# A convolution that also gathers its layer norm's sums, a norm's transpose moved into the next head, and a softmax difference in one VectorE operation

## The chip, the core and the metric

The kernel runs on one core of a Trainium2 chip. A core has TensorE (PE in the profile, its weight loads PEld), VectorE (DVE), ScalarE (ACT), GpSimd (POOL) and SyncE (SP, which here issues most DMAs). Each engine works through its own list of instructions in order and waits on semaphores for the others. The working memory is SBUF; TensorE writes to PSUM, 8 banks of 128 x 512 fp32 words each; DRAM holds inputs, outputs and what does not fit. The metric is the device time of one execution, in microseconds (us); lower is better.

## The reference, cut to what matters

One layer on 1024 tokens of 1024 channels, fp32:

```
h = rms_norm(x, g_pre);  proj = h @ w_in          # 1024 x 9216
glu_in, gate_a, q, k, v, gate_b, merge = split(proj)
u   = a * sigmoid(b)                              # a, b = halves of glu_in
u   = depthwise_causal_conv(u, 31 taps) + conv_b
y_a = (silu(layer_norm(u, ln_g, ln_b)) * silu(gate_a)) @ w_conv_proj
for 8 heads, 8 blocks of 128 queries:             # rotary on q, k; chunk mask
    p0, p1 = softmax(q0 k0), softmax(q1 k1)
    o = (p0 - lam * p1) @ v
y_b = (rms_norm(o, g_subln) * c * silu(gate_b)) @ w_attn_proj
y   = sigmoid(m_a) * y_a + sigmoid(m_b) * y_b
out = x + rms_norm(y @ w_out, g_post)
```

The layer norm is over the channels of one token, so it needs the convolution of all 1024 channels before any of it can be finished.

## The kernel before

Channels lie on partitions, 8 blocks of 128; tokens lie along the free dimension in two halves of 512. Every fp32 matrix product is made of two-part splits: a factor is cast to a reduced format (ACT) and the rest subtracted from it (POOL), and `product` (L242) does three matmuls of 128 x 512 for each of 4 slices, 12 for a product.

**Stage 1, the input projection.** Two 128-column blocks of `w_in` make a pair; there are 32 pairs, and `PLAN` (L63) lists them: u (both halves of the gated unit, block i), q (queries and keys), s and g (the two SiLU gates), v, m (merge gate of the convolution branch). A pair is done in Strassen's manner with 7 products ("steps") where 8 would be usual. `quarters` is that sequence: a step fills a PSUM bank of tag "g" (6 banks), then DVE's `plus` (L524) combines the bank with a running sum in one of 7 SBUF buffers ("cmb"), and a `use_...` function takes each finished quarter further, mostly by way of small tiles of 128 x 512. The factors of the next pair are made meanwhile (`factors`, `made`: ACT casts, POOL sums and differences, 8 buffers "wf"). For the first three pairs the two products that need no later data are begun beforehand (`begin_pair`), so these pairs have 5 steps left.

All small tiles come from `small()`, a ring of 6 buffers of one tag. They are handed out in the order in which the program is written: the n-th small tile can be written only when the (n-6)-th has been read for the last time.

**The convolution.** When both halves of u block i are there, `conv(i)` is written at the end of `quarters` for that pair. It is 31 DVE operations of 128 x 1024, one per tap: the first (L445) starts an accumulator in PSUM, 29 go on with it and the last (30 operations at L448) writes the result to an SBUF tile of its own, `cv`, which is stored to DRAM; POOL adds it to a running total (L455). The whole of it stands under a priority offset that tells the scheduler to slip the taps in where DVE would have nothing else.

**The layer norm.** PLAN's tokens l0 to l4. l0 and l1 (`ln_half`) read the stored convolution again, subtract the mean that a matmul with a constant matrix gives (L477), store the difference to `cc`, square it and add up (L472 among them). l2 (`ln_rows`) turns the sums into reciprocal roots by way of DRAM. l3 and l4 (`ln_out`) read `cc` and the stored gate `ga` back, multiply, apply SiLU and store `zd`.

**Stage 2, attention.** 8 heads of 8 query blocks in pairs (j). Per block: score matmuls (L839, L840), row maxima (DVE), exponentials (ACT, L852), then the difference of the two maps: reciprocal factors (DVE, L859), ACT scales the second map (L861), POOL adds it to the first (L862); TensorE transposes the result (L868), and after every two blocks it is multiplied with v (L881). Pieces of other products fill gaps (`filling`: `merge_gate`, L707, `conv_out`, `attn_out`). At a head's end the roots of its norm are computed, transposed on TensorE (L900), and stored; the next head's j = 0 reads them back and multiplies (`norm_head`).

**Stage 3** is the output projection, the last norm and the residual.

The scheduler orders each engine's instructions once, at build time, by the priorities and its own model; what stands in a queue below is that fixed order.

Of the kernel before, what the change touches and what calls it, by code (L numbers as in the profile page):

```python
# [40 lines left out]
def weight_blocks():  # L41
# [11 lines left out]
    for name, off in (("v", OFF_V), ("a", OFF_A), ("b", OFF_B), ("ga", OFF_GA), ("gb", OFF_GB),  # L53
# [10 lines left out]
        "m0 m1 l0 l1 g2 m2 l2 g3 l3 m3 l4")  # L64
# [3 lines left out]
def block_kernel(ctx, tc, x, positions, vecs, conv_w, lambdas, g_subln, g_post,  # L68
# [32 lines left out]
    def psum_g():  # L101
        return ps.tile(hb, F32, name="ps_g", tag="g", bufs=6)
# [205 lines left out]
    lam = const.tile([P, 4], F32, name="lam")  # L308
# [132 lines left out]
    def conv(i):  # L441
        u = conved[i]
        acc = ps.tile(blk, F32, name="cacc", tag="cv", bufs=1)
        a = wide("cv", "cv", 1)
        nc.vector.tensor_scalar(out=acc, in0=u[:, 0:T], scalar1=cw[:, i, 0:1], scalar2=vec[:, 1, i:i + 1],  # L445
                                op0=ALU.mult, op1=ALU.add)
        for k in range(1, TAPS):
            nc.vector.scalar_tensor_tensor(out=a if k == TAPS - 1 else acc, in0=u[:, k:k + T],  # L448
                                           scalar=cw[:, i, k:k + 1], in1=acc, op0=ALU.mult, op1=ALU.add)
        nc.sync.dma_start(out=cv_dram[i], in_=a)  # L450
        if i == 0:
            ln["tot"] = wide("tot", "tot", 1)
            nc.gpsimd.tensor_copy(out=ln["tot"], in_=a)
        else:
            nc.gpsimd.tensor_tensor(out=ln["tot"], in0=ln["tot"], in1=a, op=ALU.add)  # L455


    def ln_half(hh):

        sl = halves[hh]  # L460
        both = ps.tile(blk, F32, name="mu_tot", tag="cv", bufs=1)
        mu, tot = both[:, :HALF], both[:, HALF:]
        nc.tensor.matmul(mu, ones_d, ln["tot"][:, sl], start=True, stop=True)
        for i in range(8):
            c = small("cvr")
            nc.sync.dma_start(out=c, in_=cv_dram[i][:, sl])
            nc.vector.tensor_tensor(out=c, in0=c, in1=mu, op=ALU.subtract)
            nc.sync.dma_start(out=cc_dram[i][:, sl], in_=c)
            sq = small("csq") if i else tot
            nc.scalar.activation(out=sq, in_=c, func=AF.Square)  # L470
            if i:
                nc.vector.tensor_tensor(out=ln["tot"][:, sl] if i == 7 else tot, in0=sq, in1=tot, op=ALU.add)  # L472

    def ln_rows():
        for hh in range(2):
            pm = psum_g()
            nc.tensor.matmul(pm, ones_d, ln["tot"][:, halves[hh]], start=True, stop=True)  # L477
            row = small("row")
            nc.scalar.copy(out=row[0:1, :], in_=pm[0:1, :])
            nc.sync.dma_start(out=var_dram[:, halves[hh]], in_=row[0:1, :])  # L480
        vcol = tmp_pool.tile([P, 8], F32, name="vcol", bufs=1)
        vr = tmp_pool.tile([P, 8], F32, name="vr", bufs=1)
        nc.sync.dma_start(out=vcol, in_=var_dram.rearrange("o (a b) -> (o a) b", b=8))
        nc.vector.tensor_scalar(out=vcol, in0=vcol, scalar1=EPS, scalar2=None, op0=ALU.add)
        rsqrt_small(vcol, vr)
        nc.sync.dma_start(out=rs_dram.rearrange("o (a b) -> (o a) b", b=8), in_=vr)
        ln["rs"] = ps.tile(blk, F32, name="rs", tag="cv", bufs=1)
        for hh in range(2):
            rs = small("rs")
            nc.sync.dma_start(out=rs, in_=rs_dram[:, halves[hh]].broadcast_to([P, HALF]))  # L490
            nc.scalar.copy(out=ln["rs"][:, halves[hh]], in_=rs)

    def ln_out(tiles):
        for i in tiles:
            for hh in range(2):
                sl = halves[hh]
                c, g = small("cvz"), small("gaz")
                nc.sync.dma_start(out=c, in_=cc_dram[i][:, sl])
                nc.sync.dma_start(out=g, in_=ga_dram[i][:, sl])
                nc.vector.tensor_tensor(out=c, in0=c, in1=ln["rs"][:, sl], op=ALU.mult)  # L500
                nc.scalar.activation(out=c, in_=c, func=AF.Silu, scale=vec[:, 2, i:i + 1],
                                     bias=vec[:, 3, i:i + 1])
                nc.vector.scalar_tensor_tensor(out=c, in0=c, scalar=0.5, in1=g, op0=ALU.mult, op1=ALU.mult)
                nc.sync.dma_start(out=z_dram[i][:, sl], in_=c)
# [102 lines left out]
    def psum_2():  # L607
        return ps.tile(hb, F32, name="ps_r", tag="r", bufs=3)
# [202 lines left out]
    def head(h, loaded_head):  # L811
# [5 lines left out]
        for j in range(4):  # L817
# [3 lines left out]
            for u in range(2):  # L821
# [39 lines left out]
                nc.scalar.activation(out=es[1][:, :n], in_=es[1][:, :n], func=AF.Copy, scale=rz[:, 1:2])  # L861
                nc.gpsimd.tensor_tensor(out=es[0][:, :n], in0=es[0][:, :n], in1=es[1][:, :n], op=ALU.add)  # L862
# [37 lines left out]
        nc.tensor.transpose(out=rt[0:8, 0:P], in_=r, identity=ident)  # L900
# [3 lines left out]
        return nxt  # L904
# [163 lines left out]
```

## Time and profile before

| | us |
|---|---|
| median of 2 runs | 1429.84 (1429.42 to 1430.25) |
| profiled execution | 1432.29 |
| its span | 1430.5 |
| PE busy | 1218.6 (85%) |
| DVE busy | 929.1 (65%) |
| POOL busy | 805.4 (56%) |
| ACT busy | 577.4 (40%) |
| mean granted TensorE clock | 0.934 |

In the rows below, a group or a timeline line names engine, line of the kernel, operation, output<-inputs and shape; "x30" is how many there are of it; "[25.05 <-DVE tot L472]" is the time for which the engine had been idle ahead of it and what released it. A row of the windows gives a stretch, its length, the busy time of PE, PEld, DVE, ACT and POOL with the number of instructions, the granted clock, the DMA share and GB/s.

### The profile page before, as it was taken

The page shows a single profiled execution, that of the slowest core. Times are in us where ns is not written, and L with a number is a line of the kernel's source. Part 1 is how long each engine was busy: PE and PEld are TensorE (multiplying, and loading weights), DVE is VectorE, ACT ScalarE, POOL GpSimd, SP SyncE. Part 2 cuts the span into 40 slices and gives each one's busy share as a digit, 9 for nine tenths or more (in the row PEclk, how much of TensorE's full clock was granted, in tenths as well). Part 3 has the DMA queues.
Part 4 walks back from the last instruction along what each step waited for, and adds up shares of the span by engine and source line. Part 5 has one row for each costly group of instructions (what it writes and reads, how often), then busy time and mean ns, then how long its engine had stood idle before and what let it go on. Part 6 is the DMA issues. An engine that isn't in the chain of part 4 may idle for free.

```text
span 1430.5 us, 17209 instructions
## 1 busy us (share of the span) xinstructions
PE 1218.6 (85%) x5672; PEld 1006.9 (70%) x5672; DVE 929.1 (65%) x1485; ACT 577.4 (40%) x1127; POOL 805.4 (56%) x644
## 2 busy tenths in 40 slices
PE   3799999998999999995740799987899888979998
PEld 2578777877888877783530588876788777758686
DVE  4879998998999999234442253455645456635733
ACT  7543342332333323332331464465534555513311
POOL 4798798989888876765200333366433466745000
PEclk9899999999999999998775799987999989989999
DMA  6123434544333243444389653746657385557522
GB/s 211 62 90 113 159 137 136 171 145 142 131 103 113 101 153 135 162 153 149 122 287 246 189 148 133 191 123 218 183 177 192 121 239 160 171 172 262 170 97 88
DMA packets 98492, 223.76 MB, mean 156 GB/s; under 512 B 12274, under 2 KB 12738, under 8 KB 98404
## 3 DMA queue, kind: packets, MB, share of 16 engines
q1 hardware_dynamic: 95364, 212.95, 47.1%
q0 software_dynamic: 2320, 7.49, 1.8%
q10 hardware_dynamic: 720, 2.23, 0.4%
q8 instruction: 45, 0.74, 0.2%
q14 instruction: 43, 0.35, 0.1%
HBM read 150.23 MB, written 72.39 MB: 156 GB/s over the span
## 4 chain that ended last, share of the span: by engine, by line
PE 30%; DMA 12%; DVE 5%; ACT 3%; issue 3%; POOL 1%; SPq 1%; DVEq 0%; ACTq 0%; POOLq 0%
PE ps_g L665 8%; PE ps_g L707 5%; PE ps_r L881 3%; PE ps_s L839 2%; PE ps_s L840 2%; PE ps_o L989 2%; PE ps_o L990 2%; PE ps_o L991 2%; DMA cvr<-cv 2%; PE ps_o L665 2%; PE ps_r L868 1%; DMA ql<-qkl 1%; DMA gaz<-ga 1%; DMA qh<-qkh 1%; DMA yar<-yab 1%
## 5 line engine op out<-in xcount | busy, mean ns | idle before, releaser
L242 PE MATMUL ps_g<-T,wf 128*128 128x512 f32 x1536 | 362.2, 391 | 6.0 <-DVE u L524 5.6
L242 PEld LDWEIGHTS ps_g<-T,wf 128*128 128x128 f32 x1536 | 289.1, 189 | 68.1 <-DVE u L524 5.2
L242 PE MATMUL ps_g<-B,wf 128*128 128x512 f32 x1152 | 286.9, 402 | 20.4 <-DVE c L524 15.3
L448 DVE SCALAR_TENSOR_TENSOR cacc<-u,cw,cacc 128x1024 f32<-128x1024 f32 x232 | 297.5, 1282 | 2.9
L242 PEld LDWEIGHTS ps_g<-B,wf 128*128 128x128 f32 x1152 | 221.9, 194 | 72.8 <-DVE c L524 18.9
L183 POOL TENSOR_TENSOR wf<-wraw,wf 128x512 fp32r<-128x512 f32 x128 | 173.9, 1363 | 56.5 <-ACT wf L182 56.5
L862 POOL TENSOR_TENSOR e<-e 128x128 f32<-128x128 f32 (+3 forms) x64 | 91.1, 1424 | 139.5 <-ACT e L861 83.4
L183 POOL TENSOR_TENSOR wf<-wsum,wf 128x512 fp32r<-128x512 f32 x96 | 129.0, 1344 | 41.6 <-ACT wf L182 41.3
L643 POOL TENSOR_TENSOR wL<-wraw,wH 128x512 fp32r<-128x512 f32 x48 | 61.7, 1303 | 140.9 <-ACT wH L642 128.3
L707 PE MATMUL ps_g<-B,wH 128*128 128x512 f32 x256 | 84.2, 406 | 59.4 <-ACT wH L642 57.5
L852 ACT ACTIVATE e<-ps_s,nm 128x256 f32<-128x256 f32 (+7 forms) x128 | 94.8, 743 | 56.1 <-DVE nm L849 24.6
L182 ACT CAST wf<-wraw 128x512 fp32r<-128x512 f32 x128 | 78.2, 618 | 94.8 <-PE ps_g L242 78.7
L707 PEld LDWEIGHTS ps_g<-B,wH 128*128 128x128 f32 x256 | 48.6, 194 | 70.1 <-ACT wH L642 58.0
L524 DVE SCALAR_TENSOR_TENSOR u<-ps_g,u 128x512 f32<-128x512 f32 x96 | 65.6, 684 | 49.4 <-PE ps_g L242 49.4
L182 ACT CAST wf<-wsum 128x512 fp32r<-128x512 f32 x96 | 59.3, 618 | 92.0 <-PE ps_g L242 48.4
L839 PE MATMUL ps_s<-kst,qh 128*128 128x384 f32 (+4 forms) x192 | 72.3, 383 | 15.4 <-ACT e L852 12.2
L840 PE MATMUL ps_s<-kst,ql 128*128 128x384 f32 (+4 forms) x192 | 69.0, 365 | 2.1 <-DMA ql<-qkl 2.1
L871 DVE TENSOR_TENSOR wtL<-ps_r,wtH 128x512 fp32r<-128x512 f32 (+2 forms) x96 | 51.3, 551 | 27.2 <-ACT wtH L870 26.8
L849 DVE TENSOR_REDUCE nm<-ps_s 128x1 f32<-128x640 f32 (+3 forms) x64 | 65.2, 1020 | 1.4
L204 POOL TENSOR_TENSOR wsum<-wraw 128x512 f32<-128x512 f32 x32 | 43.0, 1344 | 38.3 <-DMA wraw<-w_in 34.4
L861 ACT ACTIVATE e<-e,rz 128x128 f32<-128x128 f32 (+3 forms) x64 | 49.7, 779 | 25.4 <-DVE rz L859 23.8
L665 PE MATMUL ps_g<-zH,wH 128*128 128x512 f32 x128 | 52.7, 411 | 7.1 <-DVE tar L690 3.4
(227 smaller groups left out, 2378.6 us busy)
## 6 DMA issues: line engine op xcount, KB each, us to landing
wraw<-w_in SPq DMA_DIRECT2D x67, 512.0 KB, 3.8
qkh<-qkH SPq DMA_DIRECT2D x32, 256.0 KB, 2.9
qkl<-qkL SPq DMA_DIRECT2D x32, 256.0 KB, 3.2
qh<-qkh SPq DMA_DIRECT2D x32, 256.0 KB, 7.9
ql<-qkl SPq DMA_DIRECT2D x32, 256.0 KB, 8.8
tbr<-tb SPq DMA_DIRECT2D x32, 256.0 KB, 3.3
sg<-th SPq DMA_DIRECT2D x16, 256.0 KB, 2.4
cv<-cv SPq DMA_DIRECT2D x8, 512.0 KB
```

The source lines that it names most:

```text
L182: nc.scalar.copy(out=f[:, 0, :], in_=src)
L183: nc.gpsimd.tensor_tensor(out=f[:, 1, :], in0=src, in1=f.bitcast(F32)[:, 0, :], op=ALU.subtract)
L242: nc.tensor.matmul(acc, f[:, l, sl], b[:, r, :], start=(start and d + n == 0), stop=False, skip_group_check=True)
L448: nc.vector.scalar_tensor_tensor(out=a if k == TAPS - 1 else acc, in0=u[:, k:k + T], scalar=cw[:, i, k:k + 1], in1=acc, op0=ALU.mult, op1= ...
L524: nc.vector.scalar_tensor_tensor(out=out, in0=acc, scalar=pos if s is None else s, in1=u, op0=ALU.mult, op1=ALU.add)
L665: nc.tensor.matmul(acc, w[l][:, sl], rhs[r][d][:, halves[hh]], start=(d - first + n == 0), stop=(d == last and n == 2))
L707: nc.tensor.matmul(acc, w[l][:, sl], f[:, r, :], start=(d + n == 0), stop=(d == 7 and n == 2))
L839: nc.tensor.matmul(sv[:, a, :], qh[:, qs], k[:, ks], start=True, stop=False)
L840: nc.tensor.matmul(sv[:, a, :], ql[:, qs], k[:, ks], start=False, stop=True)
L849: nc.vector.tensor_reduce(out=nm[:, m:m + 1], in_=sv, op=ALU.max, axis=AX.XY, negate=True)
L852: nc.scalar.activation(out=e[:, :n].rearrange("p (a b) -> p a b", a=c), in_=sv, func=AF.Exp, bias=nm[:, m:m + 1], accum_out=Z[:, i, m:m + 1])
L862: nc.gpsimd.tensor_tensor(out=es[0][:, :n], in0=es[0][:, :n], in1=es[1][:, :n], op=ALU.add)
```

## The change

1. The layer norm's first pass is folded into `conv`. All 31 taps now stay in the PSUM accumulator. Then, half by half, ACT copies it to a small tile "cv" (L457 or L464), POOL adds that to a running sum S1 (L465), it is stored, ACT squares it into another small tile (L468), and POOL adds that to S2 (L470). So a convolution takes 4 small tiles of the ring (the first one 2), where it took none. To keep the squares small, block 0's mean over its 128 channels is used as a shift: a matmul with a constant matrix on TensorE (L459), whose result is subtracted from block 0 (L461) and from the first tap of each later block (L448). The layer norm is then `ln_stats` (l0), which gets the roots out of S1 and S2 on TensorE and DVE, and `ln_half` (l1, l2), which reads `cv` and `ga` and stores `zd`; `cc` and the round trips of the variance through DRAM go, and PLAN's tail is written in another order.
2. The difference of the maps is one DVE operation (scale and add) per block.
3. The roots' transpose and store (`norm_row`) stand in the next head's j = 0, reading them back and multiplying (`norm_head`) in its j = 1.
4. "wf" has 7 buffers, where it had 8.

```diff
-        "m0 m1 l0 l1 g2 m2 l2 g3 l3 m3 l4")
+        "m0 m1 l0 l1 g2 l2 m2 g3 m3")
...
-        f = proj.tile([P, 2, HALF], F32R, name="wf", tag="wf", bufs=8)
+        f = proj.tile([P, 2, HALF], F32R, name="wf", tag="wf", bufs=7)
...
     def conv(i):
         u = conved[i]
         acc = ps.tile(blk, F32, name="cacc", tag="cv", bufs=1)
-        a = wide("cv", "cv", 1)
-        nc.vector.tensor_scalar(out=acc, in0=u[:, 0:T], scalar1=cw[:, i, 0:1], scalar2=vec[:, 1, i:i + 1],
-                                op0=ALU.mult, op1=ALU.add)
+        bias = vec[:, 1, i:i + 1]
+        if i == 0:
+            ln["S1"], ln["S2"], ln["shift"] = [wide(n, n, 1) for n in ("S1", "S2", "shift")]
+            nc.vector.tensor_scalar(out=acc, in0=u[:, 0:T], scalar1=cw[:, i, 0:1], scalar2=bias,
+                                    op0=ALU.mult, op1=ALU.add)
+        else:
+            nc.vector.scalar_tensor_tensor(out=acc, in0=u[:, 0:T], scalar=cw[:, i, 0:1], in1=ln["shift"],
+                                           op0=ALU.mult, op1=ALU.subtract)
         for k in range(1, TAPS):
-            nc.vector.scalar_tensor_tensor(out=a if k == TAPS - 1 else acc, in0=u[:, k:k + T],
-                                           scalar=cw[:, i, k:k + 1], in1=acc, op0=ALU.mult, op1=ALU.add)
-        nc.sync.dma_start(out=cv_dram[i], in_=a)
-        if i == 0:
-            ln["tot"] = wide("tot", "tot", 1)
-            nc.gpsimd.tensor_copy(out=ln["tot"], in_=a)
-        else:
-            nc.gpsimd.tensor_tensor(out=ln["tot"], in0=ln["tot"], in1=a, op=ALU.add)
...
+            nc.vector.scalar_tensor_tensor(out=acc, in0=u[:, k:k + T], scalar=cw[:, i, k:k + 1], in1=acc,
+                                           op0=ALU.mult, op1=ALU.add)
+        for hh in range(2):
+            sl = halves[hh]
+            c = small("cv")
+            if i == 0:
+                nc.scalar.copy(out=c, in_=acc[:, sl])
+                pm = psum_g()
+                nc.tensor.matmul(pm, ones_d, c, start=True, stop=True)
+                nc.scalar.mul(out=ln["shift"][:, sl], in_=pm, mul=float(D // P))
+                nc.vector.scalar_tensor_tensor(out=c, in0=pm, scalar=-float(D // P), in1=c, op0=ALU.mult, op1=ALU.add)
+                nc.gpsimd.tensor_copy(out=ln["S1"][:, sl], in_=c)
+            else:
+                nc.scalar.activation(out=c, in_=acc[:, sl], func=AF.Identity, bias=bias)
+                nc.gpsimd.tensor_tensor(out=ln["S1"][:, sl], in0=ln["S1"][:, sl], in1=c, op=ALU.add)
+            nc.sync.dma_start(out=cv_dram[i][:, sl], in_=c)
+            sq = small("csq") if i else ln["S2"][:, sl]
             nc.scalar.activation(out=sq, in_=c, func=AF.Square)
             if i:
-                nc.vector.tensor_tensor(out=ln["tot"][:, sl] if i == 7 else tot, in0=sq, in1=tot, op=ALU.add)
...
+                nc.gpsimd.tensor_tensor(out=ln["S2"][:, sl], in0=ln["S2"][:, sl], in1=sq, op=ALU.add)
...
+    def ln_half(hh):
...
+        for i in range(8):
+            c, g = small("cvz"), small("gaz")
+            nc.sync.dma_start(out=c, in_=cv_dram[i][:, sl])
+            nc.sync.dma_start(out=g, in_=ga_dram[i][:, sl])
+            nc.vector.tensor_tensor(out=c, in0=c, in1=mean, op=ALU.subtract)
+            nc.vector.tensor_tensor(out=c, in0=c, in1=rs, op=ALU.mult)
...
-                nc.scalar.activation(out=es[1][:, :n], in_=es[1][:, :n], func=AF.Copy, scale=rz[:, 1:2])
-                nc.gpsimd.tensor_tensor(out=es[0][:, :n], in0=es[0][:, :n], in1=es[1][:, :n], op=ALU.add)
+                nc.vector.scalar_tensor_tensor(out=es[0][:, :n], in0=es[1][:, :n], scalar=rz[:, 1:2],
+                                               in1=es[0][:, :n], op0=ALU.mult, op1=ALU.add)
...
             if j == 0 and h:
-                norm_head(h - 1)
-            if j == 1 and h < 7:
-                nxt = load_head(h + 1)
+                norm_row(h - 1)
+            if j == 1:
+                if h:
+                    norm_head(h - 1)
+                if h < 7:
+                    nxt = load_head(h + 1)
```

Because the scheduler orders the queues, the diff does not show where instructions end up. Three places of the fixed order follow. Numbers behind a tile's name tell its instances apart.

TensorE at the end of the first pair, u0 (its last step uses B22; the next pair, g0, begins with T2). Before:

```order
L242 MATMUL ps_g_737<-B22_527,wf_620 128x512 x3
L242 MATMUL ps_g_737<-B22_548,wf_620 128x512 x3
L242 MATMUL ps_g_834<-T2_624,wf_714 128x512
L242 MATMUL ps_g_834<-T2_628,wf_714 128x512 x3
L242 MATMUL ps_g_834<-T2_632,wf_714 128x512 x3
```

And now:

```order
L240 MATMUL ps_g_727<-B22_517,wf_610 128x512 x3
L240 MATMUL ps_g_727<-B22_538,wf_610 128x512 x3
L459 MATMUL ps_g_825<-cv_823,ones_d_196 128x512
L459 MATMUL ps_g_834<-cv_832,ones_d_196 128x512
L240 MATMUL ps_g_841<-T2_614,wf_704 128x512 x3
```

The two matmuls for the shift, which read the first convolution's result, now stand between u0's last step and g0's first.

VectorE at the beginning and through the third convolution, conv(2) (tag `cacc`; u2, u3 and c22 are the running sums of the pairs' steps). Before:

```order
L445 TENSOR_SCALAR cacc_1585<-u_1563,cw_210,vec_193 128x1024
L524 SCALAR_TENSOR_TENSOR u2_1968<-ps_g_1970,u2_1968 128x512
L409 TENSOR_TENSOR cst_1900<-cst_1900,ropet_1902 128x512
L448 SCALAR_TENSOR_TENSOR cacc_1585<-u_1563,cw_210,cacc_1585 128x1024
L524 SCALAR_TENSOR_TENSOR u3_2008<-ps_g_1991,u2_1968 128x512
L448 SCALAR_TENSOR_TENSOR cacc_1585<-u_1563,cw_210,cacc_1585 128x1024
L524 SCALAR_TENSOR_TENSOR c22_2026<-ps_g_2010,u3_2008 128x512
```

And now:

```order
L448 SCALAR_TENSOR_TENSOR cacc_1603<-u_1581,cw_200,shift_791 128x1024
L525 SCALAR_TENSOR_TENSOR u3_1865<-ps_g_1848,col_211,u2_1825 128x512
L451 SCALAR_TENSOR_TENSOR cacc_1603<-u_1581,cw_200,cacc_1603 128x1024 x2
L525 SCALAR_TENSOR_TENSOR c22_1883<-ps_g_1867,col_211,u3_1865 128x512
L451 SCALAR_TENSOR_TENSOR cacc_1603<-u_1581,cw_200,cacc_1603 128x1024 x3
L525 SCALAR_TENSOR_TENSOR u3_1865<-ps_g_1906,col_211,u3_1865 128x512
L451 SCALAR_TENSOR_TENSOR cacc_1603<-u_1581,cw_200,cacc_1603 128x1024 x2
L525 SCALAR_TENSOR_TENSOR u2_1825<-ps_g_1867,col_211,u2_1825 128x512
L451 SCALAR_TENSOR_TENSOR cacc_1603<-u_1581,cw_200,cacc_1603 128x1024 x3
L525 SCALAR_TENSOR_TENSOR u2_1997<-ps_g_1999,u2_1997 128x512
L451 SCALAR_TENSOR_TENSOR cacc_1603<-u_1581,cw_200,cacc_1603 128x1024 x20
L525 SCALAR_TENSOR_TENSOR u3_2037<-ps_g_2020,u2_1997 128x512
```

Before, single taps and combinations alternate; now the taps are interleaved with five combinations, and the last 20 stand in one row ahead of the sixth. At the other convolutions the row of taps that stands together at the end is 30 (conv 0), 6, 16, 16, 15, 8 and 11 (conv 1 and 3 to 7).

SyncE at the end of stage 1 (z rows are the layer norm's output, sg7 a gate of the last g pair, `wraw` the first weights and `kst` the first keys of stage 2). Before:

```order
L499 DMA gaz_6012<-ga7_103 128x512
L504 DMA zd7_147<-cvz_6003 128x512
L504 DMA zd7_147<-cvz_6011 128x512
L641 DMA wraw_6042<-w_in 128x512
L641 DMA wraw_6046<-w_in 128x512
L769 DMA kst_6078<-qkh0_64 64x1024
```

And now:

```order
L391 DMA ta4_108<-th_5776 128x512
L507 DMA zd7_139<-cvz_5628 128x512
L386 DMA sg7_95<-th_5859 128x512
L386 DMA sg7_95<-th_5895 128x512
L386 DMA sg6_94<-th_5899 128x512
```

The layer norm's last store now stands ahead of the last g and m pairs' stores; before, it stood behind all of them, directly ahead of the first loads of stage 2's weights.

More of the change, by code (lines that the diff above doesn't have):

```diff
@@ L306, in block_kernel @@
                                                               op=ALU.subtract)
-    lam = const.tile([P, 4], F32, name="lam")
+    lam = const.tile([P, 3], F32, name="lam")
     ltmp = begin.tile([P, 2, HD], F32, name="ltmp")
@@ new lines, in ln_stats @@
+    def ln_stats():
+        pm = psum_g()
+        for n, name in enumerate(("S1", "S2")):
+            for a in range(8):
+                c = 16 * n + 2 * a
+                nc.tensor.matmul(pm[:, c:c + 2], ln[name][:, a * P:(a + 1) * P], ones_d[:, 0:2], start=True, stop=True)
+        const_cols = small("cols")
+        lnr = tmp_pool.tile([P, 8], F32, name="lr", bufs=1)
+        mean, var, r = [const_cols[:, 8 * n:8 * n + 8] for n in range(2)] + [lnr]
+        nc.vector.tensor_copy(out=mean, in_=pm[:, 0:16:2])
+        nc.vector.tensor_tensor(out=mean, in0=mean, in1=mean, op=ALU.mult)
+        nc.vector.scalar_tensor_tensor(out=var, in0=pm[:, 16:32:2], scalar=EPS, in1=mean, op0=ALU.add, op1=ALU.subtract)
+        rsqrt_small(var, r)
+        ln["r"] = r
@@ L458, in ln_half @@
     def ln_half(hh):
         sl = halves[hh]
-        both = ps.tile(blk, F32, name="mu_tot", tag="cv", bufs=1)
-        mu, tot = both[:, :HALF], both[:, HALF:]
-        nc.tensor.matmul(mu, ones_d, ln["tot"][:, sl], start=True, stop=True)
+        both = ps.tile(blk, F32, name="mean_rs", tag="cv", bufs=1)
+        mean, rs = both[:, :HALF], both[:, HALF:]
+        nc.tensor.matmul(mean, ones_d, ln["S1"][:, sl], start=True, stop=True)
+        for a in range(4):
+            dg = small("diag")[:, 0:P]
+            nc.vector.tensor_scalar(out=dg, in0=ident, scalar1=ln["r"][:, 4 * hh + a:4 * hh + a + 1], scalar2=float(D),
+                                    op0=ALU.mult, op1=ALU.mult)
+            nc.tensor.matmul(rs[:, a * P:(a + 1) * P], ones_d, dg, start=True, stop=True)
@@ L464, in ln_half @@
         for i in range(8):
-            c = small("cvr")
+            c, g = small("cvz"), small("gaz")
             nc.sync.dma_start(out=c, in_=cv_dram[i][:, sl])
[L467 to L504, printed above, removed]
+            nc.sync.dma_start(out=g, in_=ga_dram[i][:, sl])
@@ L511, in ln_part @@
         else:
-            ln_out(range(4 * n - 12, 4 * n - 8))
+            ln_half(n - 1)
     USED = ("B11", "T2", "T3", "T1", "B21", "T4", "B22")
@@ L893, in head, with norm_row @@
             if j == 0 and h:
-                norm_head(h - 1)
-            if j == 1 and h < 7:
-                nxt = load_head(h + 1)
-        r = tmp_pool.tile([P, 8], F32, name="orr", bufs=2)
+                norm_row(h - 1)
[4 more added lines that the diff above has]
+                    nxt = load_head(h + 1)
+        r = roots[h] = tmp_pool.tile([P, 8], F32, name="orr", bufs=2)
         rsqrt_small(var, r)
+        return nxt
+    roots = {}
+    def norm_row(h):
         rt = psum_2()
-        nc.tensor.transpose(out=rt[0:8, 0:P], in_=r, identity=ident)
+        nc.tensor.transpose(out=rt[0:8, 0:P], in_=roots.pop(h), identity=ident)
         row = side("row")
@@ L913, in block_kernel @@
         nxt = head(h, nxt)
+    norm_row(7)
     norm_head(7)
```

16 lines of the change are left out of this document (8 added, 8 removed).

## The prediction

> **What bounds the kernel now.** I read the page's slices first, then a table of windows by stage, the waits of TensorE, and timelines where TensorE stands.
>
> ```profile
> PE   3799999998999999995740799987899888979998
> DVE  4879998998999999234442253455645456635733
> 100.00:560.00 460.00, 440.64 (x1926) 361.16 (x1925) 442.09 (x440) 159.76 (x274) 389.69 (x297) 0.99 0.39 132
> 560.00:640.00 80.00, 78.77 (x357) 64.98 (x358) 31.42 (x41) 28.75 (x50) 53.36 (x42) 1.00 0.44 147
> 640.00:732.00 92.00, 64.65 (x265) 50.75 (x263) 41.98 (x72) 31.56 (x52) 29.22 (x24) 0.85 0.50 169
> 732.00:789.00 57.00, 0.00 (x0) 0.00 (x0) 15.79 (x24) 11.86 (x17) 0.00 (x0) 0.54 0.89 263
> 789.00:1283.00 494.00, 431.09 (x2248) 365.37 (x2248) 256.34 (x658) 248.55 (x551) 238.77 (x198) 0.93 0.59 172
> ```
>
> TensorE bounds the projection: it is busy for 440.64 of 460 us from 100 to 560, although VectorE is just as full (442.09), because the taps lie beside the matmuls. Three places idle: 19.4 us in that stretch, 27.4 us around the layer norm (92.00 - 64.65), and the 57 us between the stages. In attention TensorE idles 63 us (494.00 - 431.09). The rows that show where it stands:
>
> ```profile
> PE ps_g L242 <- DVE c L524: 15.3, 7, 3.9
> 81.68 11.50 PE L242 MATMUL ps_g<-T,wf 128*128 128x512 f32 x50
> 689.42 2.07 PE L477 MATMUL ps_g<-tot,ones_d 128*128 128x512 f32 x2 [25.05 <-DVE tot L472]
> 690.51 5.55 PE L242 MATMUL ps_g<-B,wf 128*128 128x512 f32 x12
> 704.06 2.88 PE L242 MATMUL ps_g<-B,wf 128*128 128x512 f32 x12
> 706.78 2.88 PE L242 MATMUL ps_g<-T,wf 128*128 128x512 f32 x12
> 728.56 3.02 PE L242 MATMUL ps_g<-B,wf 128*128 128x512 f32 x12
> 789.13 1.22 PE L707 MATMUL ps_g<-B,wH 128*128 128x512 f32 x2 [57.55 <-ACT wH L642]
> ```
>
> The first is from the waits between 60 and 640 us (total, count, longest): there TensorE waits little for VectorE's combinations. From the starts 704.06 and 706.78 a step of 12 matmuls takes 2.72 us, a pair of 7 steps 19.0 us. Behind the 25 us of standing, a step took 5.55 us: a restart costs 5.55 - 2.88 = 2.7 us more.
>
> ```profile
> 83.55 1.35 DVE L445 TENSOR_SCALAR cacc<-u,cw,vec 128x1024 f32<-128x1024 f32 x1
> 413.20 5.26 DVE L448 SCALAR_TENSOR_TENSOR cacc<-u,cw,cacc 128x1024 f32<-128x1024 f32 x4
> 418.37 0.69 DVE L524 SCALAR_TENSOR_TENSOR u<-ps_g,u 128x512 f32<-128x512 f32 x1
> L416 ACT CAST qkH<-u 128x512 fp32r<-128x512 f32 x12 | 7.5, 621 | 26.0 <-DVE u L524 15.4 <-issue 7.1 <-POOL qkL L417 2.7
> L417 POOL TENSOR_TENSOR qkL<-u,qkH 128x512 fp32r<-128x512 f32 x12 | 15.6, 1300 | 0.0
> ```
>
> A tap takes (418.37 - 413.20) / 4 = 1.29 us, 31 taps 40 us; a combination adds 0.69. These and the two 128x512 operations of ACT (0.62) and POOL (1.30) price the stalls below.
>
> **The convolution becomes foreground work.** A convolution now takes four small tiles of the ring of six (the first takes two), and the ring is handed out in program order. So the small tiles of all later pairs wait for the last tap; ACT's and POOL's queues hold those pairs' work behind the evictions. Banks fill, and TensorE stops. The orders shown agree: taps stand in one row ahead of combinations that TensorE needs.
>
> *Conv 0.* g0's first step stands behind the shift's matmuls, so TensorE stands from 81.7 until 83.55 + 40 = 123.5, then ACT's two copies (1.24), the two matmuls (2 x 2.72 / 12 = 0.45) and handovers, 2.4 us together (estimate): 125.9 - 81.7 = 44.2, plus 2.7 for the restart: 47 us. Nothing else can cover it.
>
> *Conv 1.* The order puts 11 combinations between its taps (40 + 7.6 = 47.6 us), while TensorE has 20 steps to do (54.4). It is covered; but the gates and the rotary tables' operations (about 17 small ones on VectorE) come behind it, and 10 more steps wait on them. I take 14 us, between 3 and 22.
>
> *Convs 2, 3 and 4.* The convolution lasts 40 + 6 x 0.69 = 44 us. Five combinations and six banks let TensorE go on for 11 steps in conv 2 and 13 in 3 and 4 (30 to 35 us). After the last tap the next u needs 8 steps (21.8 us), behind about 6 us until the first bank comes free (two evictions and two squares, 2.5, then a cast, a POOL subtraction and a combination, 2.6, and handovers), 2.7 us of restart, and 2.4 us for the last combination and the two writes of u: 33. A period is 77 us. Its steps are 19, 21 and 21 (51.7, 57.1, 57.1), so it loses 25 + 20 + 20 = 65 us. At least (banks free at once, no restart) it is 13 + 2 x 11 = 35, at most, with 10 us to the first bank, 77.
>
> *Convs 5, 6 and 7.* From the same reckoning: 7 combinations in conv 5, then three steps and two pairs' small work, 63 us against 16 steps (43.5): 20. Conv 6, 63 against 21 steps: 6. Conv 7's tail of 11 taps with the v transposes behind it: 17 (10 to 20). The layer norm's own sums on TensorE and its first waits: 5.
>
> In all 47 + 14 + 65 + 20 + 6 + 17 + 5 = 174 us of standing. What goes is 19.4 + 1.2 (560 to 640) + 27.4 + 2.7 = 51 us. The last step of stage 1 ends not at 731.6 but at about 855: +123.
>
> The Trainium skill, "TensorE: Matmul & The Clock Gate", Part 1, says that the array runs at half clock after some 3.4 us of idleness and needs as long again, busy, to recover: a restart would then cost an estimated 1.7 us. The row at 690.51 says 2.7. By the rule eight restarts would cost 8 us less.
>
> **Edits at no cost of their own.** POOL's four additions per convolution (5.2 us) replace one of 128x1024 (about 2.4): 2.8 us more, in POOL's free time (389.69 of 460 us) and already in the wait for the first bank. A factor buffer less (7) still holds all of a pair's seven products; if ACT, held by an eviction, makes the next pair's late, that lies inside the same stalls. The first tap with a shift reads two SBUF inputs, at most 0.8 us more by L383's two rows below, once in a convolution. The `cc` stores and the second reading go from DMA queues that are 39 to 50% busy: nothing.
>
> **Between the stages.**
>
> ```profile
> 740.95 0.36 SPq L393 DMA_DIRECT2D ta<-th  x1
> 780.92 2.55 SPq L504 DMA_DIRECT2D zd<-cvz  x2
> 785.45 0.81 SPq L641 DMA_DIRECT2D wraw<-w_in  x2
> ```
>
> Stage 2's first weights are queued on SP behind the layer norm's last stores (780.92), though the projection's last store is out at 740.95. From the load (785.45) to the first matmul (789.13) are 3.7 us. In the new order the layer norm's last store lies two pairs ahead of the end, so the load follows m3's stores: tanh, store, load and cast, about 9 us (4 to 20), where 57.5 stood: -48.5. So attention begins 123 - 48.5 = 75 us later. The cover of the layer norm's loads is g2, m2, g3, m3 (76 us); 16 tiles that are read, multiplied and stored need less than the 41 us that the last stores lagged before. Head 0's loads lose their head start in that gap: +3.
>
> **Attention.**
>
> ```profile
> L861 ACT ACTIVATE e<-e,rz 128x128 f32<-128x128 f32 (+3 forms) x64 | 49.7, 779 | 25.4 <-DVE rz L859 23.8 <-DVE rq L155 0.7 <-DVE zz L891 0.4
> L862 POOL TENSOR_TENSOR e<-e 128x128 f32<-128x128 f32 (+3 forms) x64 | 91.1, 1424 | 139.5 <-ACT e L861 83.4 <-issue 27.8 <-PE ps_r L868 10.7
> L868 PE MATMUL ps_r<-ident,e 128*128 128x128 f32 x288 | 46.0, 289 | 1.5 <-POOL e L862 1.5
> L383 DVE SCALAR_TENSOR_TENSOR u<-th,u 128x512 f32<-128x512 f32 x8 | 8.6, 1081 | 0.0
> L383 DVE SCALAR_TENSOR_TENSOR u<-th,ps_g 128x512 f32<-128x512 f32 x8 | 5.4, 681 | 1.9 <-ACT th L363 1.9
> PE ps_r L900 <- DVE orr L158: 12.6, 4, 4.0
> PE ps_s L839 <- ACT e L852: 12.2, 13, 2.8
> ```
>
> ACT's scaling and POOL's addition go (2.2 us of chain per block), one VectorE operation comes. Its nearest row is L383 with both inputs in SBUF, 1081 ns for 512 columns; at the mean of 576 columns 1.22 us (estimate), 78 us in all. VectorE goes from 256 to about 334 of 494 us and stays behind TensorE. The chain is 1.0 us shorter per block, but TensorE waited for POOL's result only 1.5 us in all; what can be won is ACT's exponentials coming sooner (12.2), the wait for the roots at four heads' ends (12.6, which `norm_row` in the next head removes; its store and the reading back then have a pair of blocks between them, and for head 7 nothing changes), and some of the other idle time. I take -25: nearly these two sums. The ends are -45 (of 63 idle) and 0, if exponentials or maxima queue behind the new operation.
>
> On the 1081 beside 681 ns, the Trainium skill, "SBUF — State Buffer", says of the port pair shared by VectorE and GpSimd that a VectorE operation with two SBUF inputs and a GpSimd operation that reads SBUF lock each other out for a whole instruction. That speaks against both the new difference and the first tap with a shift; the pair of rows fits it, and by the lower price VectorE would have 64 x (1.22 - 0.77) = 29 us less to do, which changes the sum only where VectorE is the bound.
>
> **Sum.** 123 - 48.5 + 3 - 25 = +53 against the profiled execution's 1432.3: 1485. That execution lies 2.5 above the median: 1483 us.
>
> **Rivals.**
>
> *Only conv 0 stands (faster).* If tiles come free before they are missed, so that TensorE finds banks through convs 1 to 7, stage 1 loses the 47 and the layer norm's 27.7 + 2.7 go: 731.6 + 47 - 30 = 748.6; first merge matmul at 758, -31; +3 - 25: 1432 - 53 = 1379, so 1377 on the median. For it: in before, VectorE at 442 of 460 us hid all taps. Against: the rows of 15 to 20 taps in one piece, each 19 to 26 us, against six banks at 2.72. It decides when the convs behind the first lose less than about 40 us together, where I have 122 (174 - 47 - 5); below some 98 the change would still be within 2%.
>
> *The low ends (within 2%).* Conv 1 at 3, convs 2 to 4 at 35, conv 5 at 10, 6 at 0, 7 at 10, LN at 3: 108 with conv 0; -51, so 789 for the end of stage 1, +57 - 48.5 + 3 - 25 = -13: 1416 on the median, up to 1450 half way to my values.
>
> *VectorE becomes attention's bound (slower still).* With 78 us more in its queue each row maximum waits for the last difference; the gain of 25 goes, and the row `e L852` grows instead: 1508. It decides if TensorE's idle time in stage 2 stays at 63 or more.
>
> **Numbers.** Forecast 0.61, VectorE in attention 0.08, the low ends 0.17, only conv 0 0.14. The forecast's own range, with its terms' ends, is 1450 to 1520. The range of 8 in 10 takes in the low ends: 1416 to 1522; it leaves out the first rival and a tail above (stalls of 77 and 22 at their upper ends). A measurement of this kernel tells about 2%, 29 us, from no change: below 1401 is faster, above 1458 slower. Faster 0.14, same 0.17, slower 0.69.
>
> **What would show it.** Right: TensorE idle about 44 us before the shift's matmuls; gaps of 10 to 20 us in every convolution from the third to the sixth, released by VectorE or ACT behind a cacc row; g0 to m3 ending near 855; the gap before the first L707 about 9 us; no ACT L861 row; VectorE near 67% in stage 2 and TensorE's idle time there near 40. Wrong: taps again interleaved in time with TensorE above 95% busy from 160 to 600, or a weights' gap that stays at tens of us.

## The result, and the profile after

| | before | after |
|---|---|---|
| median, us (2 runs each) | 1429.84 | 1513.55 (1508.62 to 1518.47) |
| ratio, 95% interval | | 1.0585 (1.0437 to 1.0734) |
| the same, timed again beside other kernels | 1427.78 | 1511.34; 1.0585 (1.0545 to 1.0625) |
| profiled execution | 1432.29 | 1508.62 |
| its span | 1430.5 | 1506.9 |
| mean granted TensorE clock | 0.934 | 0.918 |

The change makes the kernel 5.9% slower: 84 us on the medians, 76 between the two profiled executions. The slices of the page after, TensorE and VectorE:

```profile
PE   3716989578695959849999858999689997979898
DVE  4886786949495979882218717555876669833743
```

Between the third and the eighteenth slice TensorE's row falls to 1 to 7 eight times, where before it was 8 or 9, and VectorE's row now alternates between 4 to 6 and 7 to 9: the two take turns. The windows of both kernels, cut at the end of u0's last step, at the end of stage 1, and at the first matmul of the merge gate (columns: stretch, its length, busy time of PE, PEld, DVE, ACT and POOL, granted clock, DMA share, GB/s). Before, then after:

```profile
0.00:81.68 81.68, 48.07 (x198) 37.37 (x199) 51.07 (x93) 53.59 (x95) 53.87 (x57) 0.94 0.37 127
81.68:731.58 649.90, 602.37 (x2627) 492.09 (x2625) 533.37 (x571) 225.94 (x385) 490.43 (x374) 0.97 0.41 139
731.58:789.13 57.55, 0.00 (x1) 0.00 (x1) 16.04 (x25) 11.99 (x17) 0.00 (x0) 0.54 0.89 263
789.13:1430.50 641.37, 568.13 (x2848) 477.44 (x2848) 328.67 (x798) 285.89 (x631) 261.13 (x214) 0.93 0.56 168
```

```profile
0.00:82.84 82.84, 48.97 (x196) 37.80 (x196) 51.17 (x93) 53.71 (x95) 54.42 (x57) 0.94 0.36 125
82.84:879.46 796.62, 620.67 (x2677) 504.70 (x2676) 564.30 (x592) 247.40 (x413) 511.60 (x396) 0.89 0.33 114
879.46:889.45 9.99, 0.00 (x0) 0.00 (x0) 0.69 (x1) 1.25 (x2) 0.00 (x0) 0.75 0.88 253
889.45:1506.90 617.45, 555.25 (x2848) 466.05 (x2848) 381.06 (x862) 242.66 (x567) 177.03 (x150) 0.96 0.60 180
```

So the projection is 146.7 us longer, of which 128.4 are time in which TensorE does nothing (796.62 - 620.67 against 649.90 - 602.37) and 18.3 a longer busy time (the new small matmuls, and steps at a lower clock behind each stop). The gap between the stages is 47.6 us shorter, and everything behind it 23.9 us shorter. With the 1.2 us of the first stretch that is +76.4.

Where TensorE stands, from its waits between 60 and 640 us (first three rows) and 640 and 890 us (next two; total, count, longest), and from its timeline (a row's bracket is the idle time ahead of it):

```profile
PE ps_g L240 <- ACT qkst L411: 81.5, 4, 25.1
PE ps_g L459 <- ACT cv L457: 44.4, 1, 44.4
PE ps_g L240 <- DVE u L525: 19.3, 4, 7.3
PE mean_rs L493 <- POOL S L465: 17.2, 1, 17.2
PE ps_g L708 <- DMA kst<-qkh: 10.0, 1, 10.0
127.24 3.39 PE L459 MATMUL ps_g<-cv,ones_d 128*128 128x512 f32 x4 [44.40 <-ACT cv L457]
310.03 5.05 PE L240 MATMUL ps_g<-B,wf 128*128 128x512 f32 x12 [25.06 <-ACT qkst L411]
389.62 4.55 PE L240 MATMUL ps_g<-B,wf 128*128 128x512 f32 x12 [19.72 <-ACT qkst L411]
467.80 4.71 PE L240 MATMUL ps_g<-B,wf 128*128 128x512 f32 x12 [19.20 <-ACT qkst L411]
544.39 5.49 PE L240 MATMUL ps_g<-B,wf 128*128 128x512 f32 x12 [17.48 <-ACT qkst L411]
```

Convs 2 to 5 have one such stop each (310 to 544 us), and the releaser is each time ACT's reading of a q pair's bank (`qkst`). What is ahead of it, at conv(2), on VectorE and on ACT:

```profile
278.29 26.45 DVE L451 SCALAR_TENSOR_TENSOR cacc<-u,cw,cacc 128x1024 f32<-128x1024 f32 x20
311.75 0.69 DVE L525 SCALAR_TENSOR_TENSOR u<-ps_g,u 128x512 f32<-128x512 f32 x1 [7.00 <-POOL qkL L415]
304.78 0.69 ACT L464 ACTIVATE cv<-cacc,vec 128x512 f32<-128x512 f32 x1 [19.10 <-DVE cacc L451]
305.50 0.63 ACT L468 ACTIVATE csq<-cv 128x512 f32<-128x512 f32 x1
307.27 0.60 ACT L414 CAST qkH<-c 128x512 fp32r<-128x512 f32 x1
309.29 0.69 ACT L411 ACTIVATE qkst<-ps_g,col 128x512 f32<-128x512 f32 x1 [0.90 <-POOL S L465]
```

The 20 taps run from 278.3 to 304.7. ACT has stood for 19 us before the convolution's copy, with the q pair's casts queued behind it; 4.5 us after the copy ACT reads the bank that TensorE needs (309.29), and TensorE goes on at 310.03. The ring shows in the last bracket: `qkst` is itself a small tile, and for its last 0.9 us that reading waited for POOL to have read the convolution's tile (L465), on which it doesn't depend otherwise. The other three stops have the same wait of 0.9 us.

### The profile page after: what moved, and what is told of

The parts are those of the page before. It is cut to its first block, busy times and chain, and to the rows that moved or that the text cites. A ratio compares the mean times of both kernels' runs of the same rounds, so it can differ in the third digit from the quotient of the medians.

```text
span 1506.9 us, 17093 instructions
## 1 busy us (share of the span) xinstructions
PE 1224.9 (81%) x5720; PEld 1008.5 (67%) x5720; DVE 997.2 (66%) x1547; ACT 545.0 (36%) x1077; POOL 743.1 (49%) x602
## 4 chain that ended last, share of the span: by engine, by line
PE 33%; DVE 8%; DMA 7%; issue 2%; ACT 1%; POOL 1%; SPq 1%; DVEq 0%; ACTq 0%; POOLq 0%
PE ps_g L240 7%; PE ps_g L666 7%; PE ps_g L708 5%; PE ps_r L882 3%; PE ps_s L840 2%; PE ps_s L841 2%; PE ps_o L999 2%; PE ps_o L1001 2%; PE ps_o L1000 2%; DMA cvz<-cv 1%; PE ps_r L869 1%; PE ps_o L666 1%; DMA kst<-qkl 1%; DVE e L862 1%; DVE nm L850 1%
## 5 line engine op out<-in xcount | busy, mean ns | idle before, releaser
L240 PE MATMUL ps_g<-B,wf 128*128 128x512 f32 x1152 | 296.1, 411 | 105.3 <-ACT qkst L411 81.5
L240 PEld LDWEIGHTS ps_g<-B,wf 128*128 128x128 f32 x1152 | 227.7, 200 | 159.4 <-ACT qkst L411 83.2
L451 DVE SCALAR_TENSOR_TENSOR cacc<-u,cw,cacc 128x1024 f32<-128x1024 f32 x240 | 309.0, 1288 | 6.5
L841 PE MATMUL ps_s<-kst,ql 128*128 128x384 f32 (+4 forms) x192 | 68.2, 362 | 1.6 <-DMA ql<-qkl 1.6
L862 DVE SCALAR_TENSOR_TENSOR e<-e,rz 128x128 f32<-128x128 f32 (+3 forms) x64 | 66.0, 1031 | 1.1
L871 ACT CAST wtH<-ps_r 128x512 fp32r<-128x512 f32 (+2 forms) x96 | 44.1, 480 | 30.4 <-PE ps_r L869 29.7
```

The source lines that it names most:

```text
L240: nc.tensor.matmul(acc, f[:, l, sl], b[:, r, :], start=(start and d + n == 0), stop=False, skip_group_check=True)
L451: nc.vector.scalar_tensor_tensor(out=acc, in0=u[:, k:k + T], scalar=cw[:, i, k:k + 1], in1=acc, op0=ALU.mult, op1=ALU.add)
L841: nc.tensor.matmul(sv[:, a, :], ql[:, qs], k[:, ks], start=False, stop=True)
L862: nc.vector.scalar_tensor_tensor(out=es[0][:, :n], in0=es[1][:, :n], scalar=rz[:, 1:2], in1=es[0][:, :n], op0=ALU.mult, op1=ALU.add)
```

## The experiments

The question was whether the ring of small tiles, handed out in program order, does this, or one of the other things that came with the fold: the shift, the additional work of ACT and POOL, the factor buffer. Ratios are to the kernel before, timed beside each group of runs (1432.71, 1430.96 and 1427.78 us).

**A ring of its own, and no shift.** The copy and the square of the convolution get two tiles of a tag that nothing else uses; the shift's tile makes room for them. Every convolution's first tap is again the one without a shift (not shown).

```diff
...
-            c = small("cv")
+            c = work.tile(hb, F32, name="cv", tag="cvo", bufs=2)
+            nc.scalar.copy(out=c, in_=acc[:, sl])
             if i == 0:
-                nc.scalar.copy(out=c, in_=acc[:, sl])
-                pm = psum_g()
-                nc.tensor.matmul(pm, ones_d, c, start=True, stop=True)
...
                 nc.gpsimd.tensor_copy(out=ln["S1"][:, sl], in_=c)
...
-            sq = small("csq") if i else ln["S2"][:, sl]
+            sq = work.tile(hb, F32, name="csq", tag="cvo", bufs=2) if i else ln["S2"][:, sl]
```

> The changed kernel with two edits: the convolution's small tiles (copy and square) come from a ring of their own of 2 tiles instead of the shared ring of 6, and the shift with its two matmuls is left out, which frees the 4 kB for them (the layer norm's sums are then of the unshifted convolution). No row of more than 4 taps stands together in VectorE's order. Theory (the shared ring makes the convolution foreground work): the standing of TensorE at the convolutions goes, 44 + 2.4 at conv 0, 69.7 at convs 2 to 4, 20 at conv 5, 9 at conv 6, 17 to 24 at conv 7's tail; some 19 us of waits as before the change stay: about 1350 us (1330 to 1375), ratio to before 0.945. Rival 1 (the added work itself, ACT's copies and squares and POOL's four additions, is what holds the pairs up): only conv 0's 47 us goes, about 1467. Rival 2 (a factor buffer less): likewise about 1467, since it still has 7.

Measured: 1341.92 us, ratio 0.9363 (0.9321 to 0.9404). Its slices and windows, cut as above:

```profile
PE   3889999899999998999994999987999988878997
DVE  4869998989999989874770756568666688516733
81.26:712.10 630.84, 606.79 (x2679) 497.58 (x2677) 549.50 (x590) 240.30 (x414) 516.89 (x398) 0.99 0.42 144
712.10:722.30 10.20, 0.00 (x1) 0.00 (x1) 0.69 (x1) 1.25 (x2) 0.00 (x0) 0.61 0.90 248
722.30:1344.00 621.70, 561.64 (x2848) 473.95 (x2848) 376.93 (x862) 242.95 (x567) 178.10 (x150) 0.93 0.61 179
```

TensorE does nothing for 24 us of the projection (630.84 - 606.79), where it did nothing for 176. The added work is all still there (four operations of ACT and four of POOL per convolution); it isn't the cause. This run alone doesn't tell the ring from the shift, since both went; the next one does. The version is 91 us faster than the kernel before on the medians; of the 86.5 us between the profiled spans 19 are in the projection, 47 in the gap and 20 behind it.

**The shared ring, and no shift.** Only the shift and its matmuls go; the tiles are from `small()` again.

> The changed kernel without the shift and its two matmuls, the convolution's small tiles still from the shared ring of 6. In VectorE's order the longest rows of taps are 12 for conv 0 and 15, 19, 16, 15, 15, 8, 11 for the others. Theory (ring): only conv 0's standing shrinks, from 47 to some 10 to 25 us, since its taps now lie beside g0's and u1's steps until the ring is used up; convs 1 to 7 stall as in the changed kernel: 1475 to 1500 us. If the shift were the cause of all of it, the other standing would go too: about 1350.

Measured: 1483.52 us, 1.0346 (1.0298 to 1.0395). TensorE's waits:

```profile
PE ps_g L240 <- ACT qkst L411: 74.4, 4, 21.8
PE ps_g L240 <- DVE u L517: 27.9, 4, 15.7
PE mean_rs L485 <- POOL S L457: 17.1, 1, 17.1
PE ps_g L240 <- ACT S L460: 10.0, 1, 10.0
```

The 44 us at conv 0 became 10 (last row), and the stops behind `qkst` and at the layer norm are nearly as they were (81.5 and 17.2 before); those released by `u` grew by 9. Between this run and the one above lies nothing but the ring: 142 us.

**Two tiles more in the shared ring.** The same memory, put into the common ring.

```diff
...
-        return work.tile(hb, dt, name=name, tag="th", bufs=6)
+        return work.tile(hb, dt, name=name, tag="th", bufs=8)
...
```

> As the run with the shared ring and no shift, but the shared ring has 8 tiles instead of 6: the same 4 kB that gave the convolution a ring of its own are added to the shared one. In VectorE's order the longest rows of taps are 12, 15, 18, 15, 15, 16, 8 and 11, as good as with 6. Theory (tiles handed out in program order behind a convolution that is late by priority): two tiles more let about one more pair quarter through per convolution, so little is won: 1460 to 1484 us. Rival (there are simply too few small tiles): most of the 142 us between the shared and the own ring come back, under 1400.

Measured: 1467.78 us, 1.0258 (1.0241 to 1.0276). Two tiles in the common ring are worth 16 us by the medians (13 by the ratios), two tiles in a ring of their own 142. It isn't that two tiles were lacking, it is who waits behind whom. A much larger common ring was not tried.

**The ring's cost without the fold.** To have the cause by itself: the kernel before, in which only the finished convolution takes its way to DRAM through two small tiles.

```diff
-        nc.sync.dma_start(out=cv_dram[i], in_=a)
+        for hh in range(2):
+            c = small("cvs")
+            nc.scalar.copy(out=c, in_=a[:, halves[hh]])
+            nc.sync.dma_start(out=cv_dram[i][:, halves[hh]], in_=c)
```

> The kernel before with one thing added: conv's result goes to DRAM by way of two small tiles of the shared ring (ACT copies each half, 16 copies of 0.62 us in all) instead of straight from its own tile. No fold, no shift, no attention edit. VectorE's order then has rows of 11, 14, 19, 14, 14, 14, 7 and 10 taps near the convolutions' ends. Theory (tiles of the ring handed out in program order make the convolution foreground work): the standing of about 120 to 142 us comes: 1550 to 1575 us. Rival (the added work, not the ring, costs): 10 us of ACT, 40% busy: 1431 to 1441.

Measured: 1552.37 us, 1.0873 (1.0843 to 1.0904). TensorE's waits:

```profile
PE ps_g L242 <- ACT qkst L413: 71.8, 4, 22.7
PE ps_g L242 <- DVE u L527: 36.3, 6, 14.0
PE ps_g L480 <- DVE tot L475: 24.6, 1, 24.6
PE mu_tot L466 <- POOL tot L458: 17.7, 1, 17.7
280.28 0.69 ACT L413 ACTIVATE qkst<-ps_g,col 128x512 f32<-128x512 f32 x1 [0.60 <-DMA cv<-cvs]
```

Sixteen copies of 0.6 us cost 125 us: the same four stops behind `qkst` as in the changed kernel, with no shift, no new sums and 8 factor buffers. The last row has the ring again: `qkst` waited for the store that reads a convolution's tile, at the four stops 2.4 us in all. The 24.6 us in the third row are not new: the kernel before has 25.05 at the same matmul.

**The shift, with the convolution's own ring.** The ring of its own as in the first run; the shift stays, and the memory comes from the factor buffers.

```diff
-        f = proj.tile([P, 2, HALF], F32R, name="wf", tag="wf", bufs=7)
+        f = proj.tile([P, 2, HALF], F32R, name="wf", tag="wf", bufs=6)
```

> The changed kernel with the convolution's small tiles in a ring of their own of 2, the shift kept, and the 4 kB taken from the factor buffers (6 instead of 7). In VectorE's order conv 0 still stands as 30 taps in a row, all others in rows of at most 4. Theory: the standing at conv 0 stays (44 to 47 us), that at convs 2 to 7 goes: about 1350 + 47 = 1397 us, if a further factor buffer less costs nothing. Rival 2 (a factor buffer less is what stalls TensorE): slower than the changed kernel, over 1514. Rival 1 (added work): as the changed kernel, about 1510.

Measured: 1419.16 us, 0.9899 (0.9852 to 0.9945), 22 us above what I had expected. The stop at conv 0 is there (first row), but TensorE also waits longer for VectorE's `u` later on, 24.5 us where it was 5.6 without the shift:

```profile
PE ps_g L459 <- ACT cv L457: 43.4, 1, 43.4
PE ps_g L240 <- DVE u L525: 24.5, 5, 11.1
84.00:160.00 76.00, 34.27 (x140) 26.93 (x141) 52.82 (x49) 13.82 (x24) 23.59 (x21) 0.71 0.13 42
```

Either the shift costs more than its stop, or the sixth buffer costs something. So the run without the shift was repeated with 6 factor buffers.

> As the run with the convolution's own ring and no shift (1342 us), but with 6 factor buffers instead of 7. It splits the 77 us between that run and the one with the shift and 6 buffers (1419). If the shift's 47 us at conv 0 are all that the shift costs, the other 30 are the sixth buffer's: 1372. If the shift costs more than conv 0 (the convolutions start later, and the first taps read two SBUF inputs), it stays near 1342 to 1350.

Measured: 1343.82 us, 0.9382 (0.9361 to 0.9404), as with 7. The seventh buffer is not missed without the shift, and the shift costs about 75 us in this setting. Of the 77 between the two profiled spans, 11 lie behind the gap, where both kernels have the same code; that part is not explained. The window of the run with the shift, above, shows where the rest may come from: from 84 to 160 us VectorE is busy for 53 us of 76; without the shift it was busy for 74.81 of them (first row below). These 22 us of taps are missing later, in a stretch in which VectorE is as full as TensorE (second row, also without the shift). That they come back as waits of TensorE is an argument; no run shows it by itself.

```profile
84.00:160.00 76.00, 76.00 (x337) 62.98 (x336) 74.81 (x81) 29.62 (x50) 60.30 (x47) 1.00 0.32 111
360.00:460.00 100.00, 94.96 (x411) 77.77 (x410) 95.47 (x90) 36.10 (x65) 86.11 (x68) 0.98 0.33 112
```

**The shift without a bank of the ring of banks.** If only the bank (also handed out in program order) held TensorE at conv 0, the shift could be had for nothing:

```diff
-                pm = psum_g()
+                pm = acc[:, sl]
                 nc.tensor.matmul(pm, ones_d, c, start=True, stop=True)
```

> As the run with the convolution's own ring, the shift and 6 factor buffers (1419 us), but the shift's two matmuls write into the convolution's own PSUM accumulator, whose half has just been copied, and no longer into a bank of the ring of 6. On TensorE's order they stand some 370 rows later, behind g0 and u1; VectorE's order has the taps of conv 0 interleaved, those of conv 1 and conv 7 in rows of 30. Theory (a bank that is taken in program order behind conv 0 is what makes TensorE stand there, and VectorE's 23 us idle meanwhile come back later as waits of TensorE): both go, 75 us less, as without the shift, 1344, or up to 1375 with conv 1's and 7's rows. Rival (the shift's chain itself holds the later convolutions up): 1400 or more.

Measured: 1470.18 us, 1.0295 (1.0262 to 1.0329): a miss, and the rival was right. The stop at conv 0 is gone, and two others took its place:

```profile
PE ps_g L479 <- POOL S L465: 60.1, 1, 60.1
PE ps_g L240 <- DVE u L381: 43.4, 1, 43.4
340.15 1.02 PE L459 MATMUL cacc<-cv,ones_d 128*128 128x512 f32 x2
350.46 39.71 DVE L451 SCALAR_TENSOR_TENSOR cacc<-u,cw,cacc 128x1024 f32<-128x1024 f32 x30
390.94 4.88 PE L240 MATMUL ps_g<-T,wf 128*128 128x512 f32 x12 [43.44 <-DVE u L381]
```

As background work the shift comes late: ACT had copied conv 0's first half at 146.9, but TensorE's order has the first of the shift's matmuls only at 340. Conv 1 has to wait for it, and its taps come in one row at 350 us, with a u tile's write (L381) behind them for which TensorE waits. At the other end, conv 7 comes as a row of 30 taps too, and the layer norm's matmul on its sums (L479) stands ahead of g2's in TensorE's order, which waits 60 us for it. These two stops are 104 of the 126 us by which it is slower than without a shift. Here, a value that every later convolution needs could not be background work.

**Attention's edits alone**, in the kernel before: both together, then each by itself. The first diff is the difference, the second the next head.

```diff
-                nc.scalar.activation(out=es[1][:, :n], in_=es[1][:, :n], func=AF.Copy, scale=rz[:, 1:2])
-                nc.gpsimd.tensor_tensor(out=es[0][:, :n], in0=es[0][:, :n], in1=es[1][:, :n], op=ALU.add)
+                nc.vector.scalar_tensor_tensor(out=es[0][:, :n], in0=es[1][:, :n], scalar=rz[:, 1:2],
+                                               in1=es[0][:, :n], op0=ALU.mult, op1=ALU.add)
```

```diff
             if j == 0 and h:
-                norm_head(h - 1)
+                norm_row(h - 1)
...
+            if j == 1:
+                if h:
+                    norm_head(h - 1)
...
```

> The kernel before with the attention's two edits alone: the difference of the maps as one VectorE operation, and the roots' transpose and store in the next head's j = 0. Theory: the gain of 24 us seen between the first merge matmul and the end (641.4 to 617.4 us) comes from these edits alone and not from the fold: 1430 - 24 = 1406 us, ratio 0.983. Rival: a part of it comes from the shorter layer norm tail (its stores no longer delay head 0's loads, less DRAM traffic): 1412 to 1420.

Measured: 1411.01 us, 0.9843 (0.98 to 0.9887): 22 us, between the 1406 of the theory and the rival's 1412. The gain comes without the fold; the interval (1404 to 1417 us) leaves room for a few us of the rival.

> The kernel before with the one VectorE operation for the difference of the maps and nothing else. By the prediction's terms about half of the 22 us that both attention edits gave alone: the wait of TensorE for the exponentials (12.2) shrinks, the wait for the roots (12.6) stays: 1433 - 10 = 1423 us. Rival (the difference gives all of it, the roots' wait is filled by other work): 1411.

Measured: 1418.85 us, 0.9915 (0.9895 to 0.9935): 12 us.

> The kernel before with the roots' transpose and store moved to the next head's j = 0 and nothing else: the wait for the roots (12.6 us at four heads' ends) goes: 1433 - 12 = 1421 us. Rival (it's a wait that other stalls replace): within 3 us of before.

Measured: 1427.27 us, 0.9974 (0.995 to 0.9998): 3.7 us, about as the rival had it. The wait for the roots (12.6 us before) is down to 2.3, and others have grown, such as this one (0.5 before):

```profile
PE ps_r L888 <- DVE og L885: 6.4, 3, 3.1
```

Twelve and four add up to 16, both together gave 22; the intervals (about 3 us for each alone, 6 for both) don't tell these apart.

## Why the prediction was right, and where its sizes were off

The direction, the mechanism and most terms held; the time came out 30 us above the predicted 1483, inside the range of 1416 to 1522 but near its upper end. The changed kernel's profiled execution lies 5 us below its median where that of before lay 2.5 above its own: this makes 7 of the 30. The other 23 are in the sum, +76 in place of +53.

- **Conv 0** (47 us): 44.40 us of standing, predicted 44.2, and the restart; g0's first step begins at 130.03, 47.2 after u0's last ended. Right.
- **Conv 1** (14): stops of 6.15, 1.08, 1.81 and 1.59 us around 218 to 266, and slower steps behind them. About right.
- **Convs 2 to 4** (65): 25.06 + 19.72 + 19.20 = 64.0, and 5.05, 4.55 and 4.71 in place of 2.88 for the first steps: 69.7. From stop to stop are 79.6 and 78.2 us, where a period of 77 was reckoned; from the last tap to the restart 5.3, reckoned 6. One part of the account was another: the first bank came free by ACT's reading of it, not by a combination on VectorE. (The 35 us given as the least for these three don't come out of their own terms: 44 + 21.8 + 2.4 = 68.2 for a period gives 39.)
- **Conv 5** (20): 17.48 + 2.6. Right. **Conv 6** (6): 7.28 and a slower step, 9.
- **Conv 7's tail and the layer norm** (17 + 5) are the terms that were mis-sized. Conv 7 cost 17.24 us of standing, then 4.79 until the v pair's copy had come through ACT, and a slow step: 24. That the first part is so near the predicted 17 is luck: the matmul that stood there is the layer norm's own (L493, waiting for POOL's sum), which the order puts ahead of the v transposes; I had only the transposes. The layer norm's small matmuls took 3.63 us for the sums and came in pieces of 0.5 to 1.2 us with waits for VectorE's `diag` between them, at 799 and from 828 to 835, and with them I count the stop at 855.76: about 15 us for 5.

```profile
679.23 1.12 PE L426 MATMUL ps_g<-ident,vst 128*128 128x128 f32 x4 [4.79 <-ACT vst L422]
787.23 3.63 PE L479 MATMUL ps_g<-ones_d,S 128*128 128x2 f32 x32
855.76 7.38 PE L240 MATMUL ps_g<-B,wf 128*128 128x512 f32 x24 [2.45 <-DVE c L525]
```

- **The end of stage 1** came at 879.5, predicted 855: 17 us of it these two terms, 8 convs 2 to 6.
- **The gap** (9 us): 9.99. The runs with attention's edits alone keep a stop of 55 to 57 us there, so the shorter gap comes from the fold's side; no run tells PLAN's other order from the shorter layer norm.
- **Attention and what follows** (+3 - 25 = -22): 617.45 against 641.37, -23.9. VectorE in 789 to 1283 was predicted at 67% busy and TensorE's idle time near 40 us. The stretch that ends as far from the kernel's end has 66% (311.00 of 469.95 us), but 50 us idle, where it was 63:

```profile
889.45:1359.40 469.95, 419.63 (x2249) 355.30 (x2250) 311.00 (x722) 205.45 (x485) 154.84 (x135) 0.95 0.64 188
```

  So the total is right, but the way there was another than I said, and about half of it is luck. TensorE's idle time behind the gap fell only from 73.2 to 62.2 us; the other 12.9 came as a shorter busy time for the same 2848 matmuls (568.13 to 555.25) at a higher granted clock (0.93 to 0.96), which no term of the sum foresaw. Why the clock was higher there is open: the run with its own ring and no shift has the same attention code and 0.93, 561.64 busy. With that same code, all that follows the gap took from 612.6 to 623.5 us in the kernels that were run, so a term of this kind can't be told to a few us. The wait for the roots, which I had counted as a gain of 12.6, was worth 3.7 by itself, and the waits for head 0's loads are 5.4 us where they were 5.0, not 3 longer.

Of the rivals, "only conv 0 stands" is what the kernel would have been with the convolution's tiles elsewhere and the shift kept: 1419 us (with 6 factor buffers), not the 1377 I had given it, perhaps since the stop at conv 0 also costs VectorE its early start. "VectorE becomes attention's bound" did not happen: TensorE's idle time there fell, and the waits for the exponentials went from 12.2 to 8.4 us. The restarts behind the four stops of 17 to 25 us cost 1.7 to 2.6 us. The estimate from the Trainium skill, "TensorE: Matmul & The Clock Gate", Part 1, was 1.7, and the row of before 2.7; the measured ones lie between.

## What to carry to other kernels

A tile from a ring that is handed out in program order ties together everything that uses the ring. Work that is to run in the background needs small tiles of its own, two of them were enough here, and nothing in the foreground should depend on its result: the shift cost 75 us with a bank of the foreground's ring, and more with a place of its own. Before a fold of this kind is judged, look in the order for the longest row of one background instruction. In these kernels rows of 8 to 30 taps went with stops of 7 to 60 us; the row shows where a stall will be, and only roughly how long.

## What the runs showed of the hardware

The new difference on VectorE was costed at 1.22 us from a row with two inputs in SBUF; its mean was 1.03. It has no one price: 896 columns took 1.14 or 1.15 us in four of eight places, but 4.14 and 4.44 in two. On VectorE and GpSimd at the first of them (the last row is an undisturbed one):

```profile
1099.06 4.14 DVE L862 SCALAR_TENSOR_TENSOR e<-e,rz 128x896 f32<-128x896 f32 x1
1098.53 1.27 POOL L644 TENSOR_TENSOR zL<-wraw,zH 128x512 fp32r<-128x512 f32 x1
1099.75 1.28 POOL L798 TENSOR_TENSOR og<-og,orb 128x512 f32<-128x512 f32 x1
1100.98 1.26 POOL L644 TENSOR_TENSOR zL<-wraw,zH 128x512 fp32r<-128x512 f32 x1
1209.71 1.14 DVE L862 SCALAR_TENSOR_TENSOR e<-e,rz 128x896 f32<-128x896 f32 x1
```

GpSimd has three operations back to back, to 1102.24; VectorE's ends at 1103.20, 0.96 us later, a little less than its own undisturbed length. In the other place GpSimd also has three, with the 0.58 us issue of a DMA ahead of the third; the last ends at 1269.53 and VectorE's at 1270.48, 0.95 later. So, as far as GpSimd's spans are exact, it got hardly anything done until GpSimd had finished, not one but three operations. The Trainium skill, "SBUF — State Buffer", section "Who interferes with whom", has this as an exclusive lock held for a whole instruction; that a row of GpSimd operations can keep VectorE out for 3 us is what these rows add. No wait of TensorE is put down to these operations; ACT's exponentials waited for them for 21.5 us in 14 places.
